# A hybrid decoder layer on one core: attention by pairs of kv groups, mixer outputs stored as high and low parts, a second feed-forward block without plain products

## The chip, the cores and the metric

The kernel runs on one core of a Trainium2 chip. The metric is the device time of one execution in microseconds. TensorE is called PE here, VectorE DVE, ScalarE ACT, GpSimd POOL and SyncE SP. SP issues nearly all DMAs.

## The reference

One inference step of one decoder layer in float32, for 1024 prompt positions and 8 sampled positions (1032 columns in all), model width 1024, feed-forward width 2816:

```
x = x + 1/2 * SwiGLU_1(RMSNorm(x))
p = RMSNorm(x) @ w_in_mix
A = sliding-window attention: 8 q heads, 2 kv groups, head size 64, window 128, ALiBi, sinks
B = gated DeltaNet: 4 heads, 128x128 state, short conv on q/k/v, gate z
x = x + concat(A, B) @ w_out_mix
x = x + 1/2 * SwiGLU_2(RMSNorm(x))
y = RMSNorm(x)
```

Besides y the step returns the new k and v rows, the convolution's last rows and the DeltaNet states.

## The kernel before

Activations lie transposed: the 1024 model features are 8 tiles of 128 partitions, the 1032 positions are columns. Each large product is made of three fp32r matmuls: both operands are split into a high part (a cast by ACT) and a low part (a subtraction by DVE or POOL), and high x high, high x low and low x high are accumulated (`mm3`, L321 to L323, and `product`, L528 to L530). Small products (attention, DeltaNet) are fp32 matmuls through `mmul` (L243) and `tr` (L248); an fp32 matmul shows in the profile as two instructions. Nearly all other operations go through a helper and show as L89.

PE runs in the order in which the program issues its instructions. The program plans that order itself: every call of `mm3` or `product` advances a clock of its own (`tick`) and lets background generators (attention blocks, DeltaNet heads, norms) issue their next step when a simple model of the other engines says that their operands are ready. The constants `PAD...` are slacks of that model. Weight operands are prepared by builders that `adv` moves on.

The stages:

- Feed-forward block 1 (about 0 to 740 us in the profile). The first `HEAD[0]` = 4 of 22 column blocks are plain products on scaled but not normalized x (`ffn_head`; the norm's factor is applied to the result), the others use seven products of half-size blocks instead of eight (`ffn_in`, with operands from `x_ops` and `w_ops`, 7 products x 4 k tiles x 3 matmuls for each half of the columns). Then the out-projection (`ffn_out`).
- In-projections of the mixer (`mix_in`): k and v, two pairs of q tiles, and for each of the four DeltaNet heads k, q, v and z. In the background run the attention (`attn_prompt`: for each of 8 blocks of 128 queries and each of the two kv groups, two q heads at a time: two score products, softmax, four transposes, two value products), the DeltaNet heads (`gdn`, `gdn_sample`) and their outputs (`emit`).
- Attention and heads 0 and 1 are written to a scratch tensor `scr` in HBM as fp32. During the last z projection four of its tiles are loaded again on SP's queue and split by ACT and DVE or POOL; heads 0 and 1 follow in `mix_out`. Heads 2 and 3 are split straight into SBUF tiles.
- Out-projection of the mixer (`mix_out`) in two passes (`PASSES`): six of eight input tiles for all columns, then the last two for one quarter of the columns (258) at a time. In the last pass each finished part is scaled and split (`cb2`, `xg_split`) for the plain products of the second block, and its squares are summed for the norm.
- Feed-forward block 2: as block 1, with `HEAD[1]` = 3 plain blocks; while they run, `prepare` normalizes x and `x_ops` builds the seven operands of each half.

SBUF work space is 44 slots of one tile each, handed out and freed by the program; a generator that finds too few free waits (`need`, `room`), and a call in the main line lets time pass until one is free.

Of the kernel before, what the change touches and what calls it, by code (L numbers as in the profile page):

```python
# [14 lines left out]
ALU = mybir.AluOpType  # L15
# [22 lines left out]
HEAD = (4, 3)  # L38
ZXY = (0, 1, 2, 1, 0, 1, 2)
# [4 lines left out]
ATT_GENS = 4  # L44
# [13 lines left out]
MIX_POOL = 3  # L58
# [3 lines left out]
PER = {2: 4, 4: 2, 6: 1}  # L62
PASSES = ((0, 6, 1), (6, 2, 0))
# [51 lines left out]
class Net:  # L115
# [120 lines left out]
    def wait(self, *jobs):  # L236
        while any(j in self.bg for j in jobs):
            self.tick(200.0)

    def mmul(self, out, lhsT, rhs, start=True, stop=True):  # L240
        n = int(np.prod(rhs.shape[1:]))
        self.now += max(110.0, n * 4 / 2.4)
        self.nc.tensor.matmul(out, lhsT, rhs, start=start, stop=stop)  # L243
# [197 lines left out]
    def x_ops(self, blk, n, out, keep=0):  # L441

        tt = self.nc.gpsimd.tensor_tensor
        b11, b12, b21, b22 = blk
        yield from self.room(2, keep)
        self.op_x(b11, n, out)
        yield True
        yield from self.room(4, keep)
        t1, t2 = self.bt([P, n], s="t1"), self.bt([P, n], s="t2")
        tt(t1, b12, b11, ALU.subtract)  # L450
        self.fr(b11)
        tt(t2, b22, t1, ALU.subtract)
        self.op_x(t2, n, out)
        yield True
        yield from self.room(2, keep)
        self.op_x(t1, n, out)
        self.fr(t1)
        yield True
        yield from self.room(2, keep)
        tt(b12, b22, b12, ALU.subtract)  # L460
        self.op_x(b12, n, out)
        self.fr(b12)
        yield True
        yield from self.room(2, keep)
        self.op_x(b21, n, out)
        yield True
        yield from self.room(2, keep)
        tt(b21, b21, t2, ALU.subtract)
        self.fr(t2)
        self.op_x(b21, n, out)  # L470
        self.fr(b21)
        yield True
        yield from self.room(2, keep)
        self.op_x(b22, n, out)
        self.fr(b22)
        yield True

    def w_ops(self, s1, s2, n, out, limit):
# [17 lines left out]

        yield from self.room(1)
# [3 lines left out]
        yield from op(r1[:, a])  # L501
        yield from op(st[:, b])
        yield from op(st[:, a])
        tt(r2[:, a], r1[:, a], r2[:, a], ALU.subtract)
        yield from op(r2[:, a])
        yield from op(r1[:, b])
        yield from op(r2[:, b])
        self.fr(r2)
# [3 lines left out]
        self.fr(r1)  # L512

# [22 lines left out]
    def swiglu(self, i, banks, d, hd, f, p):  # L536
# [10 lines left out]
        if i == 1:  # L547
            tt(t[:, 2], x, t[:, 0], ALU.add)
        elif i == 3:
            tt(t[:, 1], x, t[:, 0], ALU.add)  # L550
            tt(t[:, 1], y, t[:, 1], ALU.add)
        elif i == 4:
            nc.scalar.activation(sg, z, AF.Silu)
        elif i == 5:
            tt(t[:, 0], x, t[:, 0], ALU.add)
            nc.gpsimd.tensor_tensor(t[:, 0], t[:, 0], sg, ALU.mult)
        elif i == 6:
            tt(t[:, 2], y, t[:, 2], ALU.add)
            nc.scalar.activation(t[:, 2], t[:, 2], AF.Silu)
            nc.gpsimd.tensor_tensor(t[:, 1], t[:, 1], t[:, 2], ALU.mult)  # L560
            nc.sync.dma_start(hd[:, f, 2 * p * HW:(2 * p + 2) * HW], t[:, 0:2].rearrange("p a b -> p (a b)"))
            self.fr(t)
# [16 lines left out]
    def ffn_ops(self, w_in, head, parts=1):  # L579
        self.wops = [[] for _ in range(NF)]  # L580
        flat = lambda ap: ap.rearrange("p k c -> p (k c)")
        self.limit = A_LIVE
        self.hold = True

        def gen():
            for f in range(NF):
# [5 lines left out]
                else:  # L592
                    while f > head and self.hold:
                        yield False
# [56 lines left out]
    def ffn_in(self, xT, hd, tail, head):  # L651

        steps = [(head, (0,)), (head, (1,))] + [(f, (0, 1)) for f in range(head + 1, NF)]
        left = [[2] * 7 for _ in range(NF)]
        for f, ps in steps:
            if f > head:
# [102 lines left out]
    def x_blocks(self, get, p):  # L759

        xs = []
        for kh in range(2):
# [21 lines left out]
    def prepare(self, p, xs, acc, gi, out, rs, done, sq=None):  # L784
# [7 lines left out]
        def use(bcs, c0, w):  # L792
            l = c0 // HW
            nc.scalar.copy(rs[:, (2 * p + l) * HW:(2 * p + l + 1) * HW], bcs[:, :w])
            done.add((p, l))
# [6 lines left out]
        for ok in self.x_ops([xs[0][0], xs[0][1], xs[1][0], xs[1][1]], 4 * HW, out):  # L802
# [42 lines left out]
    def gates(self, xhi, xlo):  # L845
# [23 lines left out]
        yield PAD  # L869
# [30 lines left out]
        yield PAD  # L900
# [23 lines left out]
    def attn_prompt(self, j0, q, k, vt, scr, units):  # L924
        nc = self.nc
        for b, kv in units:
            r = slice(kv * 64, kv * 64 + 64)
            nk = P if b == 0 else 2 * P
            k0 = 0 if b == 0 else (b - 1) * P
            h0 = kv * 4 + j0  # L930
            yield from self.need(3)
            buf = self.bt([P, 1026], s="S")
            S = buf[:, :514].rearrange("p (g k) -> p g k", g=2)
            nc.scalar.copy(S[:, :, nk], self.negsink[:, h0:h0 + 2])
            ps = self.pps()
# [3 lines left out]
            for g in range(2):  # L939
                o = ps[:, g * 256:g * 256 + nk]  # L940
                nc.vector.scalar_tensor_tensor(S[:, g, :nk], self.dist[:, 2 * P - nk:], 2.0 ** -(h0 + g + 1), o, ALU.mult, ALU.subtract)
            nm = self.t("nm", [P, 2], bufs=4)
            nc.vector.tensor_reduce(nm, S[:, :, :nk + 1], AX.X, ALU.min)
            l = self.t("l", [P, 2], bufs=4)
            for g in range(2):
                nc.scalar.activation(S[:, g, :nk + 1], S[:, g, :nk + 1], AF.Exp, bias=nm[:, g:g + 1], scale=-1.0, accum_out=l[:, g:g + 1])
            nc.vector.reciprocal(l, l)
            for g in range(2):
                nc.gpsimd.tensor_scalar(S[:, g, :nk], S[:, g, :nk], l[:, g:g + 1], 1.0, ALU.mult, ALU.mult)
            yield PAD_ATT  # L950
            PT = buf[:, 514:].rearrange("p (a t) -> p a t", a=2)
            nkb = nk // P
            pt = self.pps()
            for kb in range(nkb):
                for g in range(2):
                    self.tr(pt[:, kb * 256 + g * P:kb * 256 + (g + 1) * P], S[:, g, kb * P:(kb + 1) * P])
            nc.scalar.copy(PT[:, :nkb, :], pt[:, :nk * 2].rearrange("p (a t) -> p a t", a=nkb))
# [7 lines left out]
            self.fr(buf)  # L965
            yield -300.0

    def attn_sample(self, qs, ks, vs, scr):
# [73 lines left out]
        nc.store.dma_start(scr[:, 0:4, T:TT], oj)  # L1042
# [48 lines left out]
    def gdn_sample(self, h, d, scr):  # L1091
# [5 lines left out]
        yield from self.need(4)  # L1097
# [300 lines left out]
    def emit(self, d, scr, j, s, out):  # L1398
        if "mix" in d:
            hi, lo = d["mix"]  # L1400
            self.split(hi[:, s], lo[:, s], out)
        else:
            self.nc.store.dma_start(scr[:, j, s], out)
        d.setdefault("done", set()).add(s.start)

    def mix_in(self, xhi, xlo, rs, scr, jobs):
# [46 lines left out]
        def q_pair(j0, prev):  # L1453
# [7 lines left out]
            units = [(b, kv) for b in range(NB) for kv in range(2)]  # L1461
            return q, [self.spawn(self.attn_prompt(j0, q, k, vt, scr, units[i::ATT_GENS])) for i in range(ATT_GENS)]
# [34 lines left out]
        for k in range(KT):  # L1497
# [4 lines left out]
            self.fr(xhi[k], xlo[k])  # L1502
            if k == 1:
# [255 lines left out]
```

## Time and profile before

| | us |
|---|---|
| median of 3 runs | 2117.86 |
| lowest, highest run | 2113.08, 2118.07 |
| the profiled execution | 2115.43 |
| its span, first to last instruction | 2113.2 |
| mean granted PE clock | 0.973 |
| PE, DVE, ACT, POOL busy | 2024.6, 1222.1, 699.8, 594.9 |

The times of single instructions come from one profiled execution, the median from others. A matmul's own duration includes its way through the pipeline, and matmuls overlap; the pace of a stretch is its length over its matmuls. The clock is the share of full speed that was granted, on the mean of a stretch.

### The profile page before, as it was taken

How to read it: one execution, taken by the hardware profiler on the slowest of the kernel's cores; microseconds unless marked ns; L12 is line 12 of the kernel's file. 1: busy time of each engine (PE TensorE's matmuls, PEld its weight loads, DVE VectorE, ACT ScalarE, POOL GpSimd, SP SyncE). 2: the span in 40 equal slices, each digit the busy share in tenths (PEclk: the TensorE clock that was granted, in tenths of full speed). 3: DMA queues.
4: the chain of work that ended last, by engine and by line, in shares of the span. 5: the costliest groups of instructions: out<-in, count | busy, mean ns of one | idle time of the engine just before them, and what ended most of it. 6: DMA issues, size and time to landing. Idle time of an engine off the chain costs nothing.

```text
span 2113.2 us, 37138 instructions
## 1 busy us (share of the span) xinstructions
PE 2024.6 (96%) x15062; PEld 1963.6 (93%) x15062; DVE 1222.1 (58%) x2624; ACT 699.8 (33%) x1491; POOL 594.9 (28%) x517
## 2 busy tenths in 40 slices
PE   7799999999999999999999979999999999999997
PEld 6799999999999998787888869899999999999997
DVE  7755555555533544676977874685555555464335
ACT  5233333333211333545243332443333333331112
POOL 3354444341000131332211111245444444200003
PEclk7999999999999999999999979999999999999999
DMA  4112222227322221211212151221222222552112
GB/s 152 60 58 91 81 73 84 86 71 281 113 68 60 84 81 35 69 45 32 67 46 50 57 181 35 97 70 61 86 81 83 79 81 76 194 195 84 55 41 81
DMA packets 109771, 180.81 MB, mean 86 GB/s; under 512 B 35168, under 2 KB 63744, under 8 KB 109584
## 3 DMA queue, kind: packets, MB, share of 16 engines
q1 hardware_dynamic: 109568, 178.41, 26.6%
q8 instruction: 118, 1.93, 0.4%
q14 instruction: 53, 0.43, 0.1%
q0 software_dynamic: 32, 0.03, 0.0%
HBM read 135.60 MB, written 43.85 MB: 85 GB/s over the span
## 4 chain that ended last, share of the span: by engine, by line
PE 40%; DVE 8%; DMA 1%; issue 1%; SPq 1%; ACT 0%; POOL 0%; DVEq 0%; ACTq 0%; POOLq 0%
PE mm L321 6%; PE mm L322 6%; PE mm L323 6%; PE ps L528 4%; PE ps L530 4%; PE ps L529 4%; PE ps L243 3%; PE mm L528 2%; PE mm L530 2%; PE mm L529 2%; DVE conv L89 1%; DVE inv L89 1%; SPq L102 1%; DVE Tb L89 1%; DVE x L89 1%
## 5 line engine op out<-in xcount | busy, mean ns | idle before, releaser
L528 PE MATMUL ps<-xhi,wop 128*128 128x258 f32 x1480 | 421.0, 284 | 7.4 <-DVE sw L89 7.2
L530 PE MATMUL ps<-xhi,wop 128*128 128x258 f32 x1480 | 419.3, 283 | 0.0
L529 PE MATMUL ps<-xlo,wop 128*128 128x258 f32 x1480 | 419.3, 283 | 0.0
L321 PE MATMUL mm<-hhi,hi 128*128 128x344 f32 x1008 | 322.3, 320 | 0.0
L322 PE MATMUL mm<-hlo,hi 128*128 128x344 f32 x1008 | 322.3, 320 | 0.0
L323 PE MATMUL mm<-hhi,lo 128*128 128x344 f32 x1008 | 321.6, 319 | 0.0
L89 DVE TENSOR_TENSOR wop<-r,wop 128x512 fp32r<-128x512 f32 x185 | 158.5, 859 | 253.9 <-ACT wop L89 239.8
L528 PEld LDWEIGHTS ps<-xhi,wop 128*128 128x128 f32 x1480 | 280.9, 190 | 8.7 <-issue 7.2
L529 PEld LDWEIGHTS ps<-xlo,wop 128*128 128x128 f32 x1480 | 281.9, 191 | 0.0
L530 PEld LDWEIGHTS ps<-xhi,wop 128*128 128x128 f32 x1480 | 281.2, 190 | 0.0
L89 DVE SCALAR_TENSOR_TENSOR x<-mm,x 128x344 f32<-128x344 f32 x240 | 123.3, 515 | 220.0 <-PE mm L323 217.9
L89 ACT CAST hi<-raw 128x1024 fp32r<-128x1024 f32 (+1 forms) x78 | 76.7, 984 | 357.0 <-PE mm L322 327.0
L321 PEld LDWEIGHTS mm<-hhi,hi 128*128 128x128 f32 x1008 | 189.4, 188 | 0.3 <-DVE x L89 0.3
L323 PEld LDWEIGHTS mm<-hhi,lo 128*128 128x128 f32 x1008 | 189.4, 188 | 0.0
L322 PEld LDWEIGHTS mm<-hlo,hi 128*128 128x128 f32 x1008 | 189.3, 188 | 0.0
L89 POOL TENSOR_TENSOR acc<-acc,t 128x344 f32<-128x344 f32 (+1 forms) x50 | 45.5, 911 | 508.2 <-ACT t L89 495.9
L321 PE MATMUL mm<-xnhi,hi 128*128 128x344 f32 x488 | 172.1, 353 | 0.0
L528 PE MATMUL mm<-xhi,wop 128*128 128x258 f32 x592 | 167.5, 283 | 0.0
L530 PE MATMUL mm<-xhi,wop 128*128 128x258 f32 x592 | 167.2, 283 | 0.0
L529 PE MATMUL mm<-xlo,wop 128*128 128x258 f32 x592 | 167.0, 282 | 0.0
L89 ACT CAST wop<-r 128x512 fp32r<-128x512 f32 x185 | 114.7, 621 | 144.6 <-PE mm L530 77.0
L323 PE MATMUL mm<-xnhi,lo 128*128 128x344 f32 x488 | 158.6, 325 | 0.0
(320 smaller groups left out, 4607.5 us busy)
## 6 DMA issues: line engine op xcount, KB each, us to landing
r<-in_w_in SPq DMA_DIRECT2D x86, 512.0 KB, 3.6
hraw<-hd SPq DMA_DIRECT2D x44, 516.0 KB, 5.0
hd<-sw SPq DMA_DIRECT2D x74, 258.0 KB, 2.0
raw<-in_w_out SPq DMA_DIRECT2D x34, 512.0 KB, 4.0
raw<-in_w_mix SPq DMA_DIRECT2D x22, 512.0 KB, 3.6
raw<-in_w_out SPq DMA_DIRECT2D x24, 384.0 KB, 3.2
x<-in_x SPq DMA_DIRECT2D x16, 516.0 KB, 9.0
xd<-x SPq DMA_DIRECT2D x24, 172.0 KB, 1.9
```

Source lines behind the costliest of these rows:

```text
L89: return fn(out, *a, **k)
L102: return self.eng.dma_start(out, src)
L243: self.nc.tensor.matmul(out, lhsT, rhs, start=start, stop=stop)
L321: mm(ps, whi, xhi, start=start, stop=False)
L322: mm(ps, whi, xlo, start=False, stop=False)
L323: mm(ps, wlo, xhi, start=False, stop=stop)
L528: mm(ps, w[:, a], x[0][:, c], start=first, stop=False, skip_group_check=True)
L529: mm(ps, w[:, a], x[1][:, c], start=False, stop=False, skip_group_check=True)
L530: mm(ps, wlo, x[0][:, c], start=False, stop=last, skip_group_check=True)
```

## The change

Attention handles both kv groups of a block in one visit: the four score products alternate between the groups (partitions 0 to 63 and 64 to 127), the value products between the lower and upper 64 output partitions, and the result of both is split into a high and a low part. There are three attention generators instead of four. `scr` becomes two tensors, one for high and one for low parts; loads go straight into fp32r tiles, on POOL's queue, five of them (j = 0 to 4) over the tiles of the in-projection's operand as the last z projection has read them. The passes of the out-projection take five and three input tiles instead of six and two. The plain products of the second block, and the scaled splits that feed them, are left out; that block begins with two column blocks on the first half of the columns. The seven products, their operands and the sums that follow them come in another order in both blocks. The pads of the gates step are longer.

```diff
-HEAD = (4, 3)
-ZXY = (0, 1, 2, 1, 0, 1, 2)
+HEAD = 4
+ZXY = (0, 2, 1, 0, 1, 2, 1)
-ATT_GENS = 4
+ATT_GENS = 3
+PAD_GATES = 3000.0
-PASSES = ((0, 6, 1), (6, 2, 0))
+PASSES = ((0, 5, 1), (5, 3, 0))
...
+        for x in (b11, t1, t2, b21, b12, b22, b21):
+            yield from self.room(2, keep)
+            if x is b12:
+                tt(b12, b22, b12, ALU.subtract)
+            self.op_x(x, n, out)
...
-        steps = [(head, (0,)), (head, (1,))] + [(f, (0, 1)) for f in range(head + 1, NF)]
+        if head:
+            steps = [(head, (0,)), (head, (1,))]
+        else:
+            steps = [(0, (0,)), (1, (0,)), (0, (1,)), (1, (1,))]
+        steps += [(f, (0, 1)) for f in range(steps[-1][0] + 1, NF)]
...
             for g in range(2):
-                o = ps[:, g * 256:g * 256 + nk]
-                self.mmul(o, q[g][r, b * P:(b + 1) * P], k[r, k0:k0 + nk])
+                for kv, r in enumerate(R):
+                    self.mmul(ps[kv][:, g * 256:g * 256 + nk], q[g][r, b * P:(b + 1) * P], k[r, k0:k0 + nk], pair=kv)
...
             for kb in range(nkb):
-                self.mmul(po[r, :256], vt[:, k0 // P + kb, r], PT[:, kb, :], start=kb == 0, stop=kb == nkb - 1)
-            st = buf[r, :256]
-            nc.scalar.copy(st, po[r, :256])
-            nc.store.dma_start(scr[r, j0:j0 + 2, b * P:(b + 1) * P], st.rearrange("p (j t) -> p j t", j=2))
+                for kv, r in enumerate(R):
+                    self.mmul(po[r, :256], vt[:, k0 // P + kb, r], PTs[kv][:, kb, :], start=kb == 0, stop=kb == nkb - 1, pair=kv)
+            o = self.recast(buf, [P, 4, P], F32R, "o")
+            hi, lo = o[:, 0:2], o[:, 2:4]
+            po = po[:, :256].rearrange("p (j t) -> p j t", j=2)
+            self.split(hi, lo, po)
+            self.put(scr, j0, 2, slice(b * P, (b + 1) * P), o)
...
-            self.nc.store.dma_start(scr[:, j, s], out)
+            hi = self.t2(n) if n >= P else self.t("emit", [P, n], bufs=2)
+            self.split(hi.bitcast(F32R), out.bitcast(F32R), out)
+            nc.store.dma_start(scr[0][:, j, s], hi)
+            nc.store.dma_start(scr[1][:, j, s], out)
...
-            self.fr(xhi[k], xlo[k])
-            if k == 1:
-                raws = [self.bt(s="mraw") for _ in range(4)]
-                for j, raw in enumerate(raws):
-                    nc.store.dma_start(raw, scr[:, j, :])
-            if k in (3, 4, 5, 6):
-                ms[k - 3] = self.mix_split(raws[k - 3], MIX_POOL >> (k - 3) & 1)
+            if k < 5:
+                ms[k] = self.load_mix(scr, k, [self.recast(t[k], [P, TT], F32R, "m") for t in (xhi, xlo)])
+            else:
+                self.fr(xhi[k], xlo[k])
...
+    def load_mix(self, scr, j, t):
+        for i in range(2):
+            self.tc.nc.gpsimd.dma_start(t[i], scr[i][:, j, :])
+        return t
...
-                for p in range(2):
-                    x.append(self.x_blocks(lambda kh, c0: xd[:, 4 * kh:4 * kh + 4, c0:c0 + HW], p))
+                x += [], []
                 for m in range(KT):
+                    if m in (0, 3):
+                        for p in range(2):
+                            self.x_blocks(lambda kh, c0: xd[:, 4 * kh:4 * kh + 4, c0:c0 + HW], p, x[p], (m // 3,))
...
                         one(m, c, *ws[m // per], js, m % per * g * P)
-                        cb(m, c, at(m, c))
...
-        n.ffn_ops(io["w_in2"], HEAD[1])
-        n.mix_out(scr, xd, cb2, done2, gens, ms, ds)
-        n.ffn_head(xg, xg["rs"], done, hd[1], HEAD[1])
-        n.ffn_in(xT, hd[1], lambda: n.out_ops(hd[1], lambda m: xe[:, m, :]), HEAD[1])
+        n.ffn_ops(io["w_in2"], 0)
+        n.mix_out(scr, xd, done2, gens, ms, ds)
+        n.ffn_in(xT, hd[1], lambda: n.out_ops(hd[1], lambda m: xe[:, m, :]), 0)
```

## Rows read from the trace of the kernel before

**Rows 1.** The page, part 1: busy us (share of the span) xinstructions.
```profile
PE 2024.6 (96%) x15062; PEld 1963.6 (93%) x15062; DVE 1222.1 (58%) x2624; ACT 699.8 (33%) x1491; POOL 594.9 (28%) x517
```

**Rows 2.** Stretches: length, PE, PEld, DVE, ACT, POOL busy, clock, DMA share, GB/s.
```profile
800.00:1000.00 200.00, 193.84 (x1301) 159.11 (x1300) 124.16 (x381) 103.02 (x311) 55.43 (x74) 0.98 0.17 45
1000.00:1212.00 212.00, 199.81 (x1497) 187.57 (x1496) 172.80 (x588) 79.47 (x239) 34.74 (x15) 0.97 0.20 54
1212.00:1264.00 52.00, 36.58 (x183) 31.55 (x182) 39.19 (x112) 20.63 (x45) 12.12 (x5) 0.70 0.61 188
1344.00:1465.00 121.00, 109.14 (x856) 105.31 (x855) 97.41 (x193) 56.91 (x109) 56.43 (x44) 0.97 0.28 91
1600.00:1700.00 100.00, 100.00 (x835) 100.00 (x834) 53.94 (x85) 31.95 (x65) 43.94 (x40) 1.00 0.25 80
```

**Rows 3.** Groups of PE, shapes apart: count, busy us, mean ns, idle before.
```profile
L243 PE MATMUL ps<-S,vtok 128*64 128x256 f32 x120 | 26.1, 392 | 2.1 <-ACT S L89 2.1
L243 PE MATMUL ps<-ak,aq 64*128 64x256 f32 x112 | 23.7, 399 | 0.0
...
L321 PE MATMUL ps<-xghi,phi 128*128 128x258 f32 x224 | 67.9, 303 | 8.6 <-ACT xghi L89 5.1 <-DVE x L89 3.5
```

**Rows 4.** Timeline of PE in the attention: start us, length us, operation, count.
```profile
834.47 1.14 PE L243 MATMUL ps<-ak,aq 64*128 64x256 f32 x8
835.54 1.09 PE L243 MATMUL ps<-S,vtok 128*64 128x256 f32 x8
...
855.50 1.13 PE L243 MATMUL ps<-ak,aq 64*128 64x256 f32 x4
856.56 1.08 PE L243 MATMUL ps<-S,vtok 128*64 128x256 f32 x4
```

**Rows 5.** Timeline of PE, last z projection to first out-projection matmul.
```profile
1211.94 0.32 PE L321 MATMUL ps<-xnhi,hi 128*128 128x344 f32 x1
1212.10 0.32 PE L322 MATMUL ps<-xnlo,hi 128*128 128x344 f32 x1
...
1245.04 3.54 PE L243 MATMUL ps<-kn,st 128*128 128x1 f32 x16 [4.41 <-DVE qn L89]
...
1255.06 0.56 PE L321 MATMUL mm<-mhi,hi 128*128 128x258 f32 x1
```

**Rows 6.** Timelines of DVE and of POOL, same stretch and end of head 3.
```profile
1216.73 0.23 DVE L89 TENSOR_TENSOR Tb<-Tb,inv 128x76 f32<-128x76 f32 x1
...
1219.49 2.45 DVE L89 TENSOR_TENSOR Tb<-Tb,inv 128x72 f32<-128x72 f32 x1
...
1309.56 0.69 DVE L89 TENSOR_TENSOR mlo<-t,mhi 128x512 fp32r<-128x512 f32 x1 [0.69 <-ACT mhi L89]
...
1218.80 3.05 POOL L89 TENSOR_TENSOR mlo<-mraw,mhi 128x1032 fp32r<-128x1032 f32 x1 [3.94 <-ACT mhi L89]
```

**Rows 7.** DMA issues of the whole span: count, KB each, median us to landing.
```profile
x<-xe SPq DMA_DIRECT2D x8, 516.0 KB, 9.6
...
mraw<-scr SPq DMA_DIRECT2D x6, 516.0 KB, 3.7
...
gw<-in_w_gate POOLq DMA_DIRECT2D x1, 32.0 KB, 3.0
```

**Rows 8.** Groups of DVE, shapes apart, 1344 to 1480 us.
```profile
L89 DVE SCALAR_TENSOR_TENSOR xglo<-x,c_norm_g,xghi 128x258 fp32r<-128x258 f32 x32 | 17.1, 545 | 0.0
...
L89 DVE SCALAR_TENSOR_TENSOR x<-x,c_norm_g,ps 128x258 f32<-128x258 f32 x32 | 13.1, 473 | 0.3 <-ACT rs L89 0.3
...
L89 DVE TENSOR_TENSOR wop<-r,wop 128x512 fp32r<-128x512 f32 x10 | 12.0, 1203 | 6.9 <-ACT wop L89 6.8
```

**Rows 9.** Timeline of DVE: first half's last add, its first and seventh splits.
```profile
1362.51 0.41 DVE L89 TENSOR_TENSOR x<-mm,x 128x258 f32<-128x258 f32 x1
...
1387.88 1.22 DVE L89 TENSOR_TENSOR xlo<-x,xhi 128x1032 fp32r<-128x1032 f32 x1
...
1416.12 1.23 DVE L89 TENSOR_TENSOR xlo<-x,xhi 128x1032 fp32r<-128x1032 f32 x1
```

More of the change, by code (lines that the diff above doesn't have):

```diff
@@ L236, in wait, with mmul @@
     def wait(self, *jobs):
+        n = 0
         while any(j in self.bg for j in jobs):
             self.tick(200.0)
-    def mmul(self, out, lhsT, rhs, start=True, stop=True):
+            n += 1
+            if n > 5000:
+                raise MemoryError([n for _, _, n in self.owner.values()])
+    def mmul(self, out, lhsT, rhs, start=True, stop=True, pair=None):
         n = int(np.prod(rhs.shape[1:]))
-        self.now += max(110.0, n * 4 / 2.4)
-        self.nc.tensor.matmul(out, lhsT, rhs, start=start, stop=stop)
+        self.now += 15.0 if pair else max(110.0, n * 4 / 2.4)
+        self.nc.tensor.matmul(out, lhsT, rhs, start=start, stop=stop, skip_group_check=pair is not None)
     def tr(self, out, x):
@@ L495, in op @@
             yield True
+        yield from op(r1[:, a])
         yield from self.room(1)
@@ L512, in w_ops @@
         self.fr(r1)
+        yield from op(r2[:, b])
+        self.fr(r2)
     def need_op(self, ops, i):
@@ L592, in gen @@
                 else:
-                    while f > head and self.hold:
+                    while f > (head or 1) and self.hold:
                         yield False
@@ L757, in extra, with x_blocks @@
         return hi, lo
-    def x_blocks(self, get, p):
-        xs = []
-        for kh in range(2):
+    def x_blocks(self, get, p, xs, khs=(0, 1)):
+        for kh in khs:
             xs.append([])
@@ L782, in squares, with prepare @@
             self.fr(a, b)
-    def prepare(self, p, xs, acc, gi, out, rs, done, sq=None):
+    def prepare(self, p, xs, acc, gi, out, rs=None, done=None, sq=None):
         nc = self.nc
@@ L793, in use @@
             l = c0 // HW
-            nc.scalar.copy(rs[:, (2 * p + l) * HW:(2 * p + l + 1) * HW], bcs[:, :w])
-            done.add((p, l))
+            if rs is not None:
+                nc.scalar.copy(rs[:, (2 * p + l) * HW:(2 * p + l + 1) * HW], bcs[:, :w])
+                done.add((p, l))
             for k in range(KT):
@@ new lines, in attn_prompt @@
+            buf = self.bt([P, 1028], s="S")
+            Ss = [buf[:, kv * 514:kv * 514 + 514].rearrange("p (g k) -> p g k", g=2) for kv in range(2)]
+            for kv, S in enumerate(Ss):
+                nc.scalar.copy(S[:, :, nk], self.negsink[:, kv * 4 + j0:kv * 4 + j0 + 2])
+            ps = [self.pps() for kv in range(2)]
+            for g in range(2):
+                for kv, r in enumerate(R):
+                    self.mmul(ps[kv][:, g * 256:g * 256 + nk], q[g][r, b * P:(b + 1) * P], k[r, k0:k0 + nk], pair=kv)
@@ new lines, in attn_prompt @@
+            yield PAD_ATT
+            PTs = []
+            for kv, S in enumerate(Ss):
+                pt = self.pps()
+                for kb in range(nkb):
+                    for g in range(2):
+                        self.tr(pt[:, kb * 256 + g * P:kb * 256 + (g + 1) * P], S[:, g, kb * P:(kb + 1) * P])
+                PTs.append(buf[:, kv * 514:kv * 514 + 512].rearrange("p (a t) -> p a t", a=2))
+                nc.scalar.copy(PTs[kv][:, :nkb, :], pt[:, :nk * 2].rearrange("p (a t) -> p a t", a=nkb))
@@ L1096, in gdn_sample @@
         yield from self.until(d["v"][2])
-        yield from self.need(4)
+        yield from self.need(1)
         st = self.bt([P, NS, P], s="st")
@@ L1398, in emit @@
     def emit(self, d, scr, j, s, out):
+        nc = self.nc
+        n = out.shape[1]
         if "mix" in d:
@@ L1460, in q_pair @@
             self.wait(*prev)
-            units = [(b, kv) for b in range(NB) for kv in range(2)]
-            return q, [self.spawn(self.attn_prompt(j0, q, k, vt, scr, units[i::ATT_GENS])) for i in range(ATT_GENS)]
+            return q, [self.spawn(self.attn_prompt(j0, q, k, vt, scr, range(i, NB, ATT_GENS))) for i in range(ATT_GENS)]
         def after(jobs, fn):
@@ L1573, in mix_out @@
             else:
-                ws = [self.take() for _ in range(0, KT, per)]
+                last = [self.bt([P, per * g * P], F32R, n) for n in ("whi", "wlo")]
+                ws = [self.take() for _ in range(KT // per - 1)]
+                ws.append(self.extra(*last))
                 for c in range(4):
```

163 lines of the change are left out of this document (62 added, 101 removed).

## The prediction

> **What bounds the kernel now.** I read the page's first table first: TensorE (PE) is busy for 96% of the span, the next engine for 58% [rows 1]. So time goes where PE's own work goes, or where PE stands still, and an edit on another engine counts only through PE. Then the table of stretches [rows 2]: in the feed-forward stretch PE is full (835 matmuls in 100 us, 119.8 ns each, clock 1.00) with VectorE (DVE) at 54%, so there only fewer matmuls help. The losses lie between 800 and 1465 us. From 800 to 1000 (attention) PE is idle 6.2 us; from 1000 to 1212 (DeltaNet) 12.2 us, with DVE at 82%; from 1212 to 1264 (change from the in-projections to the out-projection) 15.4 us of 52; from 1344 to 1465 (last pass of the out-projection and start of the second feed-forward block) 11.9 us of 121. The mean clock of the third stretch is 0.70: with levels of 2.4 and 1.2 GHz that is 60% of 52 us, 31 us, at 1.2 GHz, of which at most 15.4 are idle; so at least 16 us of work ran at half pace and cost some 8 us more. In the last stretch 0.97 of 121 us costs 3.6 us. Both transitions together lose about 15.4 + 8 + 11.9 + 3.6 = 39 us.
>
> **Attention on PE: less.** A score product (K of 64, two fp32 halves) uses half of the array's rows, a value product half of its columns. The PE timeline shows both cases already [rows 4]: one unit alone takes 4 halves in 1.13 us and 4 in 1.08 us; where units of both kv groups happen to stand together, 8 halves take 1.14 and 1.09 us. The second group is free. The change makes that the rule: 14 block visits at 1.14 + 1.09 and two with half the keys at about half of that give 33 us, against 23.7 us for the 112 full-width score halves, some 1.7 for 16 of half the width, and 26.1 for the values now [rows 3]: 51 us. Eighteen saved by the busy time; by the starts it is 16, since busy counts a lead-in per burst. Lower bound nothing: if DVE, ACT and POOL, whose softmax work per head is unchanged, hold PE up instead. DVE is at 62% there [rows 2]. What it gains in work is one 128x256 low part per visit, 16 times about 0.41 us, 7 us (ACT drops to one copy per visit); that lies under PE's projections. I take 15, nearer to the timeline's end. The gates step has longer pads: it moves behind PE's other work and may remove a little of the 6.2 us; I count nothing.
>
> **Second feed-forward block: less.** A block of plain products is 2 x 8 x 4 x 3 = 192 matmuls (seven blocks, 1344 in both halves; one of six groups of 224 in [rows 3]); with seven products it is 7 x 4 x 3 x 2 = 168. Three blocks lose 72 matmuls at 119.8 ns: 8.6 us. Nothing hides it, PE is the bound there, and the new order of the seven products leaves their number as it is.
>
> **In-projection to out-projection: moved.** Now the last z projection starts at 1211.9 and the first out-projection matmul runs at 1255.1, 43 us later, though z is 72 matmuls 0.16 us apart, 11.5 us of work [rows 5]. PE's queue is in order and stands behind DeltaNet steps that wait for DVE (4.41 us for qn, and others). DVE is behind because six loaded mixer tiles are split there: ACT 6, DVE 4 and POOL 2, and while POOL works on one (3.05 us) a DVE step of 72 elements takes 2.45 us instead of 0.23 [rows 6]. All that goes: four DVE splits of about 1.2 us (the size of the xlo split in [rows 9]), two POOL ones that block DVE for about 2 us each: 9 us of DVE's queue, and two heads' parts come back as 4 splits of 512, some 0.7 us each, spread over the stages before. Eight x loads become four, so that PE reaches the first pass without waiting for slots. New: ten loads of 516 KB on POOL's queue, each waiting until PE has read the tile it overwrites. The third stretch moved 188 GB/s with the DMA engines 61% busy [rows 2], so some 308 GB/s is to be had; a single load of this size lands in 3.7 us [rows 7]. 5.3 MB take 17 us, from when z's first k is read, about 1.4 us after z's start: done at 1211.9 + 1.4 + 2 + 17 = 1232, some 20 us after z's start, when z with the DeltaNet steps in between has ended too. What is queued behind a waiting load is POOL's: low parts of the next weights, of which two tiles are ahead. With the waits for DeltaNet steps that stay I expect the first pass to start 25 to 35 us after z's start instead of 43, at a clock mostly held: 12 us gained of the 23 lost. Bounds: all 23 gained, or loads at the slowest rate of this size in the trace, 9.6 us (rival below). The doubled stores (hi and lo of 128x256) go through SP's queue and can hold weight loads behind them; no row shows PE waiting for weights now, so I count nothing.
>
> The Trainium skill has a rule against this step, SBUF — State Buffer, "Who interferes with whom": a DMA from the POOL queue has its descriptors written by GpSimd, and while DVE holds the shared port pair it can't write them. The trace shows POOL and DVE blocking each other (2.45 us against 0.23, [rows 6]), but its only POOL load [rows 7] belongs to the first microseconds of the program, so no run here shows the rule for a load beside a busy DVE; by it the sum would lose the 12 us, the third rival below.
>
> **Start of the second feed-forward block: cover lost.** The plain blocks needed no norm; the seven-product ones need normalized, combined operands. Gone: 32 scaled splits, 17.1 us of DVE within the last pass [rows 8], behind which PE waited for its accumulators. The last pass grows to 9 matmuls a group (one head moves to it, the first pass shrinks by as much), so 16 groups, 17.3 us, cover the first half's preparation. DVE's list from the end of that half's last add to the first operand: 16 adds (6.6 us), 4 square sums (2), 16 normalizing products (7.5), rsqrt and diagonals (3), one split (1.2), and 7 to 14 weight splits at 1.2 us (8 to 17): 28 to 37 us [rows 8, 9], against 17.3: a wait of 11 to 20 if all stand ahead, less if some weight splits come earlier or later. Then DVE has six more splits and the second half's preparation, about 20 us, beside 20 us of two half-steps: some 4 to 8 us more. Bounds 10 to 28 us; I take 17.5, against 15.5 lost in this stretch now: 2 us worse. Before, the chain from the last add to the first split took 26.6 us and to the seventh 54.8 us [rows 9], with the 17.1 us of DVE in its way.
>
> **Sum.** -15 - 8.6 - 12 + 2 = -33.6 on the profiled execution's 2115.4 us: 2081.8. The median shown is 2.4 us above that execution: 2084.
>
> **Rivals.**
> (1) DVE takes PE's place in attention and DeltaNet, or the pairs don't form as in the timeline. For it: DVE at 82% from 1000 to 1212. Against it: attention itself has 62%. Without the 15: 2099.
> (2) The entry to the second block goes at the pace of the old chain: seventh operand 54.8 us after the add, when PE has 17.3 + 10 us to do: 29 us lost instead of 17.5, 2096. Against it: the 17.1 us of DVE gone from that chain.
> (3) POOL's loads get going only when DVE's backlog ends at about 1246, 14 us later: the out-projection starts at about today's time, 2096. For it: DVE's pile-up in that stretch; against it: 9 us less of it.
> (4) Slower. The ten loads are served one after another. A load of this size from HBM takes 3.7 to 9.6 us [rows 7]; the first pass then starts 1.4 + 10 t after z. Today's start costs 43 us and about 4 more of half clock; the other terms give 21.6 us, so from t = 7.4 us on the kernel is slower by over 0.3%. At 9.6: 97 us, 50 worse, 2117.9 - 21.6 + 50 = 2146. Against it: loads on SP overlap, and the one POOL load (32 KB) landed in 3.0 us.
> (5) Everything at its good end: attention 18, transition 23, entry 5 better: 2117.9 - 55 = 2063.
>
> **How the numbers follow.** Forecast 0.52 (own range 2070 to 2096), (1) 0.15, (2) 0.10, (3) 0.10, (4) 0.06, (5) 0.07. The range 2058 to 2113 leaves out (4) and the worst pile-ups of (1) to (3), which together reach 2122, some 0.15 in all. About 0.3% (6 us) is what a measurement here can tell from no change: faster 0.82, from all cases but (4) and pile-ups of the others; same 0.08, two or three of (1) to (3) together; slower 0.10, (4) and mishaps on top of a pile-up.
>
> **What would show it.** Score and value groups on PE at about half of 51 us. 504 instead of 576 matmuls of 258 columns in the first three blocks of the second half. First out-projection matmul 25 to 35 us after z's first; if it waits for a POOL load that lands 34 us or more after z's start, (3) or (4). PE idle at the entry to the second block 10 to 28 us, released by DVE splits. Wrong would be: PE idle in 800 to 1212 rising by as much as the attention matmuls fall, or a last pass that waits for head 3 (its output ends at 1309.6 now, [rows 6], 35 us ahead of need; the shorter way to the last pass uses most of that).

## The result, and the profile after

The changed kernel takes 2122.96 us (median of 13 runs, 2117.90 to 2126.67), the kernel before 2116.56 on the same chips: ratio 1.0030, 95% interval 1.0017 to 1.0042. It is slower by 0.3%, where 2084 was forecast. The profiled execution has a span of 2118.7 us against 2113.2, and its mean clock is 0.962 against 0.973.

First the page's busy times after, for [rows 1], and the same five stretches as in [rows 2] (columns as there):

```profile
PE 2016.0 (95%) x14990; PEld 1964.4 (93%) x14990; DVE 1187.5 (56%) x2634; ACT 673.7 (32%) x1463; POOL 597.4 (28%) x539
```

```profile
800.00:1000.00 200.00, 195.05 (x1381) 166.34 (x1380) 139.68 (x449) 100.92 (x319) 52.55 (x74) 0.95 0.22 59
1000.00:1212.00 212.00, 189.65 (x1373) 178.30 (x1372) 164.39 (x542) 72.98 (x208) 31.96 (x15) 0.92 0.19 54
1212.00:1264.00 52.00, 44.95 (x355) 41.40 (x354) 36.80 (x123) 16.82 (x49) 13.57 (x16) 0.86 0.79 253
1344.00:1465.00 121.00, 98.86 (x743) 96.33 (x743) 90.52 (x163) 42.31 (x75) 60.77 (x44) 0.87 0.20 66
1600.00:1700.00 100.00, 100.00 (x835) 100.00 (x833) 45.97 (x84) 30.16 (x64) 43.04 (x40) 1.00 0.24 75
```

PE has less to do and the kernel takes longer. The idle time moved from the third stretch (15.4 to 7.1 us) into the second (12.2 to 22.4) and the fourth (11.9 to 22.1), and in both the clock fell, from 0.97 to 0.92 and 0.87. Followed by what PE has reached, in us from the span's start:

| PE reaches | before | after | ahead |
|---|---|---|---|
| first in-projection | 758.4 | 753.1 | 5.3 |
| sixth in-projection after it (attention half done) | 882.0 | 854.3 | 27.6 |
| tenth | 973.3 | 952.3 | 21.0 |
| z projection | 1211.9 | 1211.2 | 0.7 |
| first pass of the out-projection | 1255.1 | 1229.6 | 25.5 |
| last pass | 1344.3 | 1333.5 | 10.8 |
| second block | 1376.2 | 1377.6 | -1.4 |
| its fourth column block done | 1483.1 | 1488.2 | -5.1 |

The last pass holds 96 matmuls more after the change and the first 96 fewer, 11.5 us at 119.8 ns. So nothing of the out-projection's 25.5 us is left at its end.

A ledger of a stretch serves below. "Idle" is a stretch less PE's busy time; "clock" is (1 - granted clock) x busy time, summed over windows of 10 us; the rest is work at full clock. The groups of [rows 3], from the first in-projection on, are after:

```profile
L247 PE MATMUL ps<-S,vtok 128*64 128x256 f32 x120 | 18.8, 409 | 4.0 <-ACT S L89 2.9 <-DVE o L89 1.0
L247 PE MATMUL ps<-ak,aq 64*128 64x256 f32 x112 | 17.6, 417 | 0.2
```

### The profile page after: what moved, and what is told of

The parts are those of the page before. It is cut to its first block, busy times and chain, and to the rows that moved or that the text cites. A ratio compares the mean times of both kernels' runs of the same rounds, so it can differ in the third digit from the quotient of the medians.

```text
span 2118.7 us, 37131 instructions
## 1 busy us (share of the span) xinstructions
PE 2016.0 (95%) x14990; PEld 1964.4 (93%) x14990; DVE 1187.5 (56%) x2634; ACT 673.7 (32%) x1463; POOL 597.4 (28%) x539
## 3 DMA queue, kind: packets, MB, share of 16 engines
q1 hardware_dynamic: 113360, 178.41, 26.4%
## 4 chain that ended last, share of the span: by engine, by line
PE 77%; DVE 11%; DMA 2%; issue 1%; ACT 1%; SPq 1%; POOL 0%; DVEq 0%; ACTq 0%; POOLq 0%
PE mm L325 11%; PE mm L326 11%; PE mm L327 10%; PE ps L515 9%; PE ps L516 9%; PE ps L517 9%; PE ps L247 5%; PE mm L516 4%; PE mm L515 4%; PE mm L517 4%; DVE conv L89 1%; DVE inv L89 1%; PE ps L252 1%; DVE x L89 1%; DVE xlo L89 1%
## 5 line engine op out<-in xcount | busy, mean ns | idle before, releaser
L515 PE MATMUL ps<-xhi,wop 128*128 128x258 f32 x1600 | 456.2, 285 | 7.0 <-DVE sw L89 2.9
L516 PE MATMUL ps<-xlo,wop 128*128 128x258 f32 x1600 | 454.6, 284 | 5.5 <-DVE xlo L89 5.5
L517 PE MATMUL ps<-xhi,wop 128*128 128x258 f32 x1600 | 454.4, 284 | 0.0
L515 PEld LDWEIGHTS ps<-xhi,wop 128*128 128x128 f32 x1600 | 304.8, 191 | 8.4 <-DVE sw L89 3.7
L516 PEld LDWEIGHTS ps<-xlo,wop 128*128 128x128 f32 x1600 | 305.8, 191 | 6.1 <-DVE xlo L89 6.1
L517 PEld LDWEIGHTS ps<-xhi,wop 128*128 128x128 f32 x1600 | 304.9, 191 | 0.0
L516 PE MATMUL mm<-xlo,wop 128*128 128x258 f32 x640 | 182.2, 285 | 9.0 <-DVE xlo L89 9.0
L89 ACT CAST hi<-raw 128x1024 fp32r<-128x1024 f32 (+2 forms) x79 | 76.2, 965 | 336.3 <-PE mm L326 302.6
L515 PE MATMUL mm<-xhi,wop 128*128 128x258 f32 x640 | 182.0, 284 | 0.0
L517 PE MATMUL mm<-xhi,wop 128*128 128x258 f32 x640 | 181.7, 284 | 0.0
L89 ACT CAST wop<-r 128x512 fp32r<-128x512 f32 x200 | 120.6, 620 | 181.5 <-DMA r<-in_w_in 132.5
L89 POOL TENSOR_TENSOR ws<-r 128x512 f32<-128x512 f32 x40 | 52.3, 1307 | 402.4 <-DMA r<-in_w_in 375.4
```

Of the source, the lines that this page charges most:

```text
L89: return fn(out, *a, **k)
L515: mm(ps, w[:, a], x[0][:, c], start=first, stop=False, skip_group_check=True)
L516: mm(ps, w[:, a], x[1][:, c], start=False, stop=False, skip_group_check=True)
L517: mm(ps, wlo, x[0][:, c], start=False, stop=last, skip_group_check=True)
```

## Experiments

Theories at the start: **A**, the DeltaNet chain through DVE, ACT and SP sets when the out-projection can start; **B**, the loss comes from storing and loading in two parts; **C**, any change of PE's planned order moves the stretch some us either way; **D**, the clock. Each run is timed against the kernel before on its own chip. The ledger, from the first in-projection to the z projection:

| kernel | ratio (95%) | stretch | idle | clock | rest |
|---|---|---|---|---|---|
| before | | 453.6 | 19.4 | 11.0 | 423.1 |
| after | 1.0030 (1.0017-1.0042) | 458.1 | 28.6 | 26.4 | 403.1 |
| pairs_only | 1.0017 (1.0001-1.0033) | 453.9 | 23.5 | 29.9 | 400.5 |
| pairs_spread | 1.0038 (1.0022-1.0054) | 459.7 | 32.0 | 21.4 | 406.2 |
| pairs_late | 0.9996 (0.9983-1.0009) | 447.6 | 23.7 | 24.2 | 399.8 |
| pairs_gates | 1.0050 (1.0033-1.0068) | 455.1 | 35.2 | 19.7 | 400.2 |
| pairs_fill | 1.0078 (1.0059-1.0096) | 471.8 | 23.5 | 33.3 | 415.0 |
| base_light | 0.9974 (0.9961-0.9986) | 452.9 | 25.6 | 15.7 | 411.5 |
| pairs_light | 0.9842 (0.9820-0.9864) | 425.6 | 24.3 | 11.4 | 389.9 |
| change_light | 0.9844 (0.9830-0.9859) | 443.3 | 30.9 | 19.8 | 392.6 |
| base_conv | 1.0096 (1.0073-1.0118) | 486.6 | 28.2 | 32.5 | 425.9 |
| pairs_conv | 0.9985 (0.9970-1.0000) | 453.3 | 28.1 | 17.6 | 407.6 |

Each row of the ledger is one execution, the ratio is from all runs. How far executions differ shows where PE's order is the same: up to the z projection it is so in the kernel before, no_plain_only, order_only and order_dve_sums (all below), and their stretches are 453.6, 453.6, 454.3 and 448.0 us, their clock losses 11.0, 11.0, 18.0 and 9.9. Four kernels with the order of after (change_with_plain, change_hold, change_dve_sums and after itself) have 24.7 to 30.5. A clock loss that differs by less than some 8 us between two rows tells nothing.

### One part at a time

**pairs_only**: the new `attn_prompt`, `ATT_GENS` and `PAD_GATES` in the kernel before, the output copied and stored once:

```diff
+            st = buf[:, :256]
+            nc.scalar.copy(st, po[:, :256])
+            nc.store.dma_start(scr[:, j0:j0 + 2, b * P:(b + 1) * P], ...)
```

> The kernel before with the attention alone taken by pairs of kv groups (three generators, longer pads of the gates step); outputs stored as fp32 as before. Theory A (the DeltaNet chain through DVE, ACT and SP sets when the out-projection can start, so what PE saves in the attention is given back before the last z projection): projections 6 to 10 start some 15 us earlier, the z projection at about the old time, ratio 0.999 to 1.001. Rival B (the pairs keep their gain and the loss of the whole change comes from what is stored and loaded as two parts): z projection 15 us earlier, ratio 0.993. Rival C (the mainline is re-planned and any change of it moves the DeltaNet stretch by some us either way): a ratio in between or over 1.002.

The sixth in-projection after the first started 22.6 us earlier (859.4 against 882.0) and the z projection at 1212.3, as before. Work fell by 22.6 us; the clock took 18.9 of it and idle time 4.1. B is out as the main cause: the two-part stores aren't in this kernel. Where the clock went shows in windows of 10 us of this kernel:

```profile
950.00:960.00 10.00, 10.00 (x148) 8.42 (x147) 8.94 (x24) 5.79 (x11) 2.40 (x2) 1.00 0.23 69
960.00:970.00 10.00, 8.73 (x67) 7.39 (x66) 9.14 (x27) 3.40 (x6) 0.00 (x0) 0.87 0.23 66
970.00:980.00 10.00, 10.00 (x40) 7.54 (x38) 1.38 (x2) 2.62 (x14) 0.00 (x0) 0.50 0.13 52
980.00:990.00 10.00, 10.00 (x44) 9.49 (x45) 3.70 (x21) 2.73 (x15) 0.00 (x0) 0.50 0.01 2
990.00:1000.00 10.00, 10.00 (x58) 10.00 (x57) 4.84 (x28) 1.71 (x8) 0.00 (x0) 0.77 0.00 1
```

For 20 us PE is busy without a gap at 1.2 GHz, and the other engines have little to do (DVE 1.38 and 3.70 of 10). In it PE works through the sample steps of attention and head 0 with few projections between; one row of each, and the pace: a projection matmul every 0.28 to 0.29 us where it is 0.16 at 2.4 GHz [rows 5]. The pace of 0.16 is back at 994.8 us, in a row of projection matmuls that no small product interrupts.

```profile
977.81 3.58 PE L999 MATMUL ps<-attn_smp,kc 64*128 64x4 f32 x20
981.32 1.12 PE L249 MATMUL ps<-ident,conv 128*128 128x128 f32 x4
982.53 0.49 PE L323 MATMUL mm<-xnlo,hi 128*128 128x344 f32 x1
982.81 0.49 PE L324 MATMUL mm<-xnhi,lo 128*128 128x344 f32 x1
```

**no_plain_only** (`HEAD = 4` and `head == 0` in the second block, `cb2` left out), **order_only** (`ZXY`, `x_ops`, `w_ops`, `swiglu` of after, and 3 slots kept free in both blocks) and **change_with_plain** (after, with `HEAD = (4, 3)` and `cb2` put back):

> The kernel before with the plain products of the second block left out and nothing else. By the two traces the entry to that block lost 12.5 us more and saved 8.6: theory A expects about 4 us more, ratio 1.002. Rival (the loss at the entry comes from the longer last pass and the other order of the seven operands): the forecast's own price, 2 us lost against 8.6 saved, 7 us less, ratio 0.997.

> The kernel before with the other order of the seven products, of their operands and of the sums behind them, in both blocks, and nothing else. The trace after reached the first in-projection 5.3 us earlier, and only this part touches the first block: theory A expects 5 us less there, and with the same block count in the second block 0 to 5 more, ratio 0.995 to 0.9975. Rival (the 5.3 us are not from the order but from the execution): ratio 0.999 to 1.001.

> The changed kernel with three plain blocks put back at the head of the second feed-forward block, and their scaled splits in the last pass of three input tiles. Theory A (leaving out the plain blocks cost 4 us): 2119 us, ratio 1.001 to the kernel before. Rival (the entry is as late with plain blocks, since the 17 us of scaled splits stand in the longer last pass): 2123 us or more, ratio 1.003 or above.

Leaving out the plain blocks alone costs 27 us (ratio 1.0127, 1.0103 to 1.0152), far over either expectation. The order alone gains: 0.9947 (0.9928 to 0.9966), 11 us, slightly more than forecast; by the trace 7.8 of them stand before the first in-projection. Putting the plain blocks back takes some 10 us off the changed kernel (2111.91, ratio 0.9985, 0.9965 to 1.0005, against 1.0030), where either expectation had it slower than before; its fourth block is done at 1478.2 instead of 1488.2. So the order gains 11, the pairs nothing, and the missing plain blocks cost about what the order gains. Storing in two parts, the loads on POOL's queue and the new passes weren't run alone. As an estimate: order and pairs together would make 0.9964 if their ratios add up, and change_with_plain, which has these three besides, is at 0.9985; so they bring no gain that shows.

### What takes the pairs' gain

Two reliefs, each on the kernel before and on pairs: PE's small sample products thinned (eight one-column products become one of eight columns, `st[:, 0, :]` for all, and in the attention's sample step eight of four columns become one of 32), and two of three convolution taps left out on DVE (`range(1, 4)` becomes `range(1, 2)`).

> The kernel before with the small products of the sampled positions thinned out on PE alone: one product over all eight samples (with the first sample's matrix) in place of eight one-column products, in the DeltaNet sample steps and the attention's sample step. VectorE's work is unchanged. Direct saving by the rows: two groups of 3.3 us per head and some 6 us in the attention's sample step, 25 to 32 us, ratio 0.985 to 0.989, in either theory. It is the reference for the next one.

> Attention by pairs, and the same small products thinned out. Rival D (the gain of the pairs is eaten by the clock: without the attention between them the sample steps of attention and head 0 stand close together and TensorE falls to 1.2 GHz): the pairs' gain comes back, 8 to 15 us less than the run with thinned products alone, ratio to it 0.993 to 0.996. Theory A (DVE's queue sets the pace): no gain over it, 0.999 to 1.002.

> The kernel before with two of the three accumulating taps of each short convolution left out: 24 DVE instructions of 1.36 us less, 33 us, PE's work unchanged. Theory A (DVE sets the pace from 880 to the out-projection): 10 to 25 us less, ratio 0.988 to 0.995. Rival D (the clock and PE's own order): under 5 us less, 0.998 or above.

> Attention by pairs, and the same taps left out. Theory A: with 33 us less of DVE the pairs' 16 us on PE are kept, 8 to 16 us less than the run with taps left out alone, ratio to it 0.992 to 0.996. Rival D: the pairs gain nothing over it, 0.999 to 1.002.

base_light missed its forecast: it is 5 us faster than before, not 25 to 32. Its ledger has 11.6 us less work, and 10.9 more idle time and clock loss. Against it the pairs gain 28.6 us (2109.63 to 2081.03), far over D's 8 to 15: the clock loses 11.4 instead of pairs_only's 29.9, and the z projection starts at 1183. With DVE relieved by 33 us the kernel before got 20 us slower, which neither theory had: by clock (32.5) and idle time (28.2), in an execution 9 us above the median. Against that plan the pairs gain 24 us, more than A's 8 to 16 and not D's nothing; how much of it is that plan's bad luck stays open. Against pairs_only the relief gives some 7 us, though PE's idle time is larger with it (28.1 against 23.5). So in neither kernel does less work for DVE bring less idle time of PE: A as a matter of DVE's work is not borne out, and C isn't refuted. The windows of pairs_light and of pairs_fill (next) at the same place:

```profile
970.00:980.00 10.00, 10.00 (x60) 9.78 (x61) 5.92 (x51) 6.08 (x34) 0.00 (x0) 0.82 0.14 54
980.00:990.00 10.00, 10.00 (x76) 9.59 (x75) 7.31 (x22) 3.48 (x8) 2.37 (x1) 1.00 0.21 56
```

```profile
970.00:980.00 10.00, 10.00 (x39) 8.19 (x37) 1.04 (x2) 2.61 (x14) 0.00 (x0) 0.53 0.13 52
980.00:990.00 10.00, 10.00 (x41) 9.33 (x40) 1.64 (x9) 2.72 (x15) 0.00 (x0) 0.50 0.01 2
```

Then four ways to keep the clock without leaving work out: sample steps 2.5 us apart (`PAD_SMP = 2500`), the attention's sample step started five projections later, dense products between the small ones, and the old gates pad.

> Attention by pairs alone, and the sample steps of DeltaNet and attention leave 2.5 us instead of 0.4 between one another in the plan, so more projections stand between their small products. Work the same as with pairs alone. Rival D (clock): the stretch to the z projection loses 10 to 15 us of its 30 us of clock, ratio to before 0.993 to 0.996. Theory A (DVE chain) or C (any change of the order moves it some us either way): ratio 0.999 to 1.004 as for pairs alone.

> Attention by pairs alone, and the attention's sample step (kc, vc: 64 products of 4 columns) starts after head 0's z projection instead of beside head 0's scan and sample step. Work the same. Rival D: the half clock from 967 to 995 us goes, 8 to 14 us less, ratio to before 0.994 to 0.997, unless the step gathers with head 1's sample step instead. Theory A or C: 0.999 to 1.004.

> Attention by pairs alone, with filler products (128x128 by 128x344, results unused) put between the sample steps' small products of heads 0 to 2 and of the attention: some 64 more products, 10 us of work more. Rival D (the clock falls because these stretches are sparse): clock from 960 to 1020 us back from 0.77 to 0.9 or more, the stretch to the z projection loses 10 to 15 us of clock less than pairs alone, time 0 to 6 us less than pairs alone, ratio to before 0.998 to 1.002. Theory C (order alone): clock loss unchanged, 8 to 12 us more, 1.005 to 1.008.

> Attention by pairs alone, with the gates step's old pad of 0.4 us instead of 3: nothing but the order of PE's small steps changes. Theory C (any change of the order moves the stretch): clock loss and waits to the z projection differ by 5 us or more from pairs alone, ratio to before anywhere from 0.994 to 1.008. Theory A or D in their pure form: 1.000 to 1.003.

None of the four kept the gain, and each ratio came out where C had it (two of them where A had it too), not D. Spreading took 8.5 us from the clock's loss and put 8.5 on idle time; the later start gave the clock back at its place (0.98 from 960 to 1020, 0.77 in pairs_only) but only 5.7 us up to z (8.5 and 5.7 are no more than executions of one order can differ by); filling added 14.5 us of work and left the clock at 0.50 to 0.53; one pad's value moved 10 us from clock to waits. The sum of idle time and clock is 30.4 us before and 48 to 57 in the changed kernel, pairs_only and these four; in pairs_light it is 36, in base_light 41. The simple form of D, that dense columns between the small ones hold the clock, is refuted by the filler as far as 64 of them go.

**change_light**, the same thinning in the changed kernel:

> The changed kernel with the sample steps' small products thinned on PE (one product over all eight samples with the first sample's matrix). The kernel before with the same thinning took 2109.6. Rival D': the pairs' gain comes back as it did for pairs alone: 2085 to 2095, ratio to before 0.985 to 0.990. Otherwise (the hi and lo stores and loads keep the DeltaNet stretch as late as it is): only the thinned work goes, 2110 to 2118, 0.997 to 1.001.

2086.91 us: 36 less than the changed kernel and 23 less than the kernel before with the same thinning, as D' (the small products are what costs) said. The two profiled executions differ by 28: up to z by 10.5 us of work and 6.6 of clock loss, less 2.3 more idle time; another 13 us go after z. But idle time and clock up to z still sum to 51 us, 55 in the changed kernel. So in pairs_light the loss goes with the small products; in change_light the time goes and most of the loss up to z stays. That the small products are what costs is likely and not shown. What makes the clock fall in one order and hold in another stays open.

### The start of the second block

In the trace after, head 3's last step stands late (PE, ACT, DVE, POOL, rows of one timeline each):

```profile
1309.13 1.25 PE L252 MATMUL ps<-ident,t 128*128 128x128 f32 x4 [5.58 <-ACT t L89]
...
1308.71 1.14 ACT L89 ACTIVATE t<-ps,rsqy 128x128 f32<-128x128 f32 x4 [4.51 <-DVE rsqy L89]
...
1299.54 1.29 DVE L89 TENSOR_SCALAR rsqy<-rsqt 128x4 int32<-128x4 int32 x1
1301.08 1.11 DVE L89 TENSOR_TENSOR rsqt<-rsqy 128x4 f32<-128x4 f32 x1
1307.71 0.16 DVE L89 SCALAR_TENSOR_TENSOR rsqy<-rsqt,rsqy 128x4 f32<-128x4 f32 x1
...
1299.51 1.30 POOL L89 TENSOR_TENSOR ws<-r 128x512 f32<-128x512 f32 x1 [1.88 <-DVE rsqt L89]
1300.88 1.29 POOL L89 TENSOR_TENSOR ws<-ws,r 128x512 f32<-128x512 f32 x1
```

Five DVE steps on 4 columns take 1.1 to 1.5 us instead of 0.16 while POOL adds up the second block's first weights, some 5.5 us in all (the expectation of change_hold counts six). The Trainium skill (SBUF — State Buffer, "Who interferes with whom") says that a DVE step with two SBUF inputs contends with a POOL step that reads SBUF; four of the five, as the TENSOR_TENSOR at 1301.08, agree. The fifth, the TENSOR_SCALAR at 1299.54 (1.29 us), has one such input and isn't covered by that sentence. With plain blocks (change_with_plain) no such sums stand there: no wait of that kind, and the first pass takes 96.3 us instead of 103.8.

**change_hold** (the weight builder yields until the last pass begins) and **change_dve_sums** (`tt` is DVE's in `x_ops` of block 2 and in `w_ops` for f < 2):

> The changed kernel, with the second block's weight operands held back until the last pass of the out-projection begins. By the trace after, POOL's sums for them (1299 to 1305 us) slow six small DVE steps of head 3 from 0.16 to 1.1 to 1.5 us, and PE waits 5.6 us for that. Theory E (that is why the first pass took 104 us and not 96): first pass 96 to 98 us; the operands are late instead, so the entry gives back 0 to 5: ratio to before 0.999 to 1.002. Rival (the entry needs them that early): first pass shorter, entry longer by as much or more, 1.003 to 1.006.

> The changed kernel, with the sums for the second block's first two weight blocks and for its x operands on DVE instead of POOL (some 0.7 us each for 8 of 512 columns, some 1.2 for 8 of 1032: 15 us more for DVE, none of the two-engine blocking). Theory F (POOL's sums block DVE's steps, so leaving out the plain blocks costs 10 us): the wait of 5.6 us at head 3's last step goes and the entry loses 3 to 8 us less, ratio to before 0.997 to 1.000. Rival (DVE's queue at the entry is full as it is, so 15 us more for it cost more than the blocking): 1.004 to 1.009.

The hold held nothing (1.0038, 1.0022 to 1.0055): the kernel fixes the program's order for PE alone (`ORDERED`), and the sums still ran at 1303 to 1309, with a wait of 5.27 us; it tells nothing about E. With the sums on DVE the wait stayed too (4.75 us), now behind eight sums and splits of 0.69 us and some adds. So in each of these traces head 3 waits while the operands are prepared, on either engine; a run that only moves their preparation away is missing. The kernel came to 1.0001 (0.9988 to 1.0014), 6 us less than the changed one, at the edge of F's range but not for F's reason: the wait is there, and from the second block's start to the end of its fourth column block it is 2 us faster, not 3 to 8.

### Versions meant to beat both

> A version meant to beat both: attention by pairs, the changed order of the seven products, and the sample steps 2.5 us apart in the plan; stores as fp32, three plain blocks and six and two input tiles as before. Order alone gave 11 us; rival D adds 10 to 15 for the pairs once the clock holds: ratio to before 0.988 to 0.991. Theory A or C: order's 11 us alone, 0.993 to 0.997.

> A version meant to beat the order alone: pairs, the changed order of products, and the attention's sample step started after head 0's z projection. If the gains add up (0.9996 and 0.9947): 0.994 to 0.995, no better than order alone. Rival D would give 0.990.

> A version meant to beat both: the kernel before with the changed order of products, and the sums of the second block's x operands and of its first two weight blocks of seven products on DVE. Sums on DVE gave the changed kernel 4 to 6 us. If POOL's sums block DVE there too: 2 to 6 us less than order alone, ratio to before 0.992 to 0.994; if DVE's queue is what counts: 0.995 to 0.999.

With pairs: 0.9965 (0.9948 to 0.9983) and 0.9980 (0.9968 to 0.9993), both slower than the order alone; the first came out where A or C had it, the second above both its expectations. **order_dve_sums** is the best of the kernels that leave nothing out: 2095.30 us, ratio 0.9890 (0.9874 to 0.9906), 21 us less than before and 28 less than the change, and a larger gain than forecast. From the first plain product to the end of the fourth block, before, in order_only and in this kernel (columns as above):

```profile
1376.00:1483.00 107.00, 98.65 (x783) 97.63 (x783) 76.69 (x137) 39.55 (x65) 55.43 (x37) 0.95 0.20 65
```

```profile
1369.00:1474.00 105.00, 97.19 (x779) 96.11 (x778) 76.78 (x136) 39.42 (x66) 52.51 (x36) 0.97 0.21 64
```

```profile
1365.00:1463.00 98.00, 95.35 (x780) 94.68 (x779) 78.39 (x152) 39.24 (x66) 30.49 (x21) 0.98 0.21 68
```

The same matmuls, 9 us sooner than before; about 2 of these are the order's, 7 the sums'. DVE's busy time hardly grows (1.6 us against order_only) when 22 us of POOL's busy time go. The means by shape in these stretches say why: a sum of 1032 columns takes 1.22 us on DVE where POOL took 2.4, and DVE's other steps get shorter, the splits of sums of weights (`wop<-ws`) 0.68 us instead of 1.31, the diagonals (`t<-ident,rsqy`) 0.29 instead of 0.71. The other 5 us between the two medians' ratios (0.9947 and 0.9890) aren't explained by this stretch.

## Why the prediction was wrong, step by step

**Attention, -15.** The saving was there: the two groups fell from 49.8 to 36.4 us busy (not to half, and some halves ran at 1.2 GHz), the ledger's work by 20.0. What failed is the step from there to the time: "nearer to the timeline's end" took PE's saved time as time saved. The text named what would be wrong, idle time of PE rising in 800 to 1212. It rose by 8.9 us (18.4 to 27.3), and the clock took more than the rest (15.4 up to z), for which the forecast had no term. Rival (1) had the outcome, but its engine isn't borne out: DVE is 78% busy from 1000 to 1212, less than before, and relieving it left more idle time, not less.

**Second block, -8.6.** The count is as forecast: 672 matmuls stand there in place of 744, up to the end of the fourth column block.

**Transition, -12.** The moves worked better than forecast. The first pass began 18.4 us after z (25 to 35 forecast, 43.1 before), and rivals (3) and (4) are refuted by the loads' own rows (POOL's issues, durations in ns, then the time to landing):

```profile
L1529 POOL DMA_DIRECT2D m<-scr_lo x5: 530/530/595, 1213.8 to 1219.7; - x5
L1529 POOL DMA_DIRECT2D m<-scr_hi x5: 530/537/547, 1214.4 to 1220.5; - x5
...
DMA to landing us min/median/max: 5.1/8.0/11.3
```

They landed in 5.1 to 11.3 us side by side, with DVE 17.8 of 19 us busy from 1211 to 1230. What failed is taking the first pass's start for the gain. DeltaNet steps that PE used to wait for ahead of that pass now stand in it: 480 matmuls, 57.5 us of work, took 103.8 us; before 576, 69 us of work, took 89.1. The idle time in that pass rose from 0.2 to 11.4 us, the clock's loss from 4.3 to 12.3. From z's start to the last pass 132.4 us became 122.3, less than the 11.5 us moved out; from z's start to the second block 164.2 became 166.4. In place of 12 us gained stand 2 lost.

**Entry, +2.** Mis-sized, at its upper bound of 28 us: 110.7 us for 80.5 us of matmuls, 30 lost against 17.8 by the pace (26.9 against 12.4 as idle time and clock). This is rival (2)'s outcome (29 lost; its own numbers give 27.5). PE waits for the splits of x, as foreseen; DVE is full there, POOL full or half, and the clock falls with the waits (after):

```profile
1380.00:1390.00 10.00, 5.00 (x23) 4.79 (x23) 10.00 (x5) 3.06 (x3) 10.00 (x5) 0.66 0.13 45
1410.00:1420.00 10.00, 2.76 (x19) 2.31 (x18) 9.52 (x19) 3.15 (x3) 5.43 (x4) 0.65 0.07 28
```

```profile
1384.64 0.58 PE L516 MATMUL mm<-xlo,wop 128*128 128x258 f32 x1 [5.35 <-DVE xlo L89]
1419.37 0.58 PE L516 MATMUL ps<-xlo,wop 128*128 128x258 f32 x1 [5.08 <-DVE xlo L89]
...
1376.92 1.22 DVE L89 TENSOR_TENSOR xlo<-x,xhi 128x1032 fp32r<-128x1032 f32 x1
1381.19 4.99 DVE L89 TENSOR_TENSOR xlo<-t,xhi 128x1032 fp32r<-128x1032 f32 x2
...
1380.68 2.81 POOL L89 TENSOR_TENSOR x<-x,x 128x1032 f32<-128x1032 f32 x1
```

The list of DVE's work there left out POOL's sums, beside which two splits of x take 4.99 us instead of 2.4, and head 3's late step. With the plain blocks put back the change is some 10 us faster: leaving them out cost about 10, and was forecast to gain 6.6. Of these 10, 7.5 stand in the first pass (103.8 us against 96.3), where the forecast had no term.

**Order of the products, 0.** "Leaves their number as it is" was true and beside the point: it gains 11 us, most of it where block 1 passes from plain to seven products (its fifth column block is done at 157.8 us instead of 165.4, order_only against before).

Added up: the spans differ by +5.5 where -33.6 was forecast, 39 us. Of these the stretch to the z projection has 24.6 (idle 9.2, clock 15.4), the transition 14 (2 lost, 12 gained in the forecast), the entry 10.5 (12.5 more lost, 2 forecast); the larger saving of work (20, not 15) and the order's 5.3 before the first in-projection take off 10. That makes 39. Shown are the places and the amounts; why PE's idle time and clock loss up to z grew with the pairs stays open.

## What to carry to other kernels

Work taken from a busy in-order engine is a gain only if what stands between its waits afterwards still fills them: make the ledger of idle time, clock loss and work for the stretch, and price all three. Take a mixed change apart on the chip; here its one plain winner, an order of products, had been priced at nothing and hid a loss of the same size. Preparation that is pulled ahead of its use lands in someone else's queue; moving two-input sums from POOL to the DVE that they blocked went with another 0.6% beside the order's 0.5%. And compare executions of one order before reading a ledger: here the clock alone moved it by 8 us.

## What was not expected of the hardware

- TensorE ran at 1.2 GHz with no gap in its busy time for 20 us (970 to 990 in pairs_only, 10.00 of 10 in both windows). The Trainium skill (TensorE: Matmul & The Clock Gate, "HAM oscillation — how this bites in real kernels") tells of a clock that falls when PE waits between bursts; here PE's longest wait in the 25 us before was 1.3 us.
- In the kernel before, each unit issues its two score products one after the other, not alternating with the other group's, and where units of both groups meet 8 halves still took 1.14 us [rows 4], with starts in twos, 0.01 to 0.02 us apart (834.47 and 834.49, 834.79 and 834.81). Whether the alternation in the program is needed wasn't tried in the changed kernel.
